# Where the first norm of token blocks 2 and 3 is taken: by tokens in place of by features

## The chip, the core and the metric

The program runs on one core of one Trainium2 chip. The metric is the device time of one execution in microseconds (us), taken as a median over runs. The core has a matrix engine (TensorE, PE in the profile), a vector engine (VectorE, DVE), a scalar engine (ScalarE, ACT), a general engine (GpSimd, POOL), and an engine that issues the transfers between HBM and the on-chip memory (SyncE, SP). The matrix engine writes into PSUM banks; everything else stays in SBUF tiles of 128 partitions.

## The reference

One layer of an encoder: stick-breaking attention (16 heads of 64) and a SwGLU feed-forward part, both between RMS norms and with shift, scale and gate from a conditioning vector. S = 2048 tokens, D = 1024 features, float32. The change touches only the first line:

```python
def rms_norm(x, g):
    return x * lax.rsqrt(jnp.mean(x * x, axis=-1, keepdims=True) + EPS) * g

h = modulate(rms_norm(x, norm_g[0]), sh_m, sc_m)      # h * (1 + scale) + shift
q, k, v = split(h @ w_qkv)
for each 128-token block:
    z = q k^T / 8;  sp = softplus(z) below the diagonal;  rest = reverse cumsum(sp)
    o = exp(z - rest) @ v
x = x + gate * rms_norm(o @ w_o, norm_g[1])
x = x + gate * rms_norm(swiglu_ffn(modulate(rms_norm(x, norm_g[2]), ...)), norm_g[3])
```

## The kernel before

**Tiling.** The tokens lie in four blocks of 512 (0 to 3), the heads in eight pairs p, the features in eight slices k of 128. Each float32 product is made of three matmuls over a high and a low half (`mm3`, L198 to L200): high by high, high by low, low by high. One product of a projection is a chain of 8 slices, 24 matmuls of 128x512, into one PSUM bank (`pj`).

**Steps.** The attention phase is a list of steps (p, b). `project` (L472) makes for each step three products: t=1 (keys), t=0 (queries), t=2 (values), in this order. The first steps are (0,0), then (1,0), which is "parked" (its keys, queries and values are written to HBM as `k_park`, `q_park`, `v_park` and read back later), then (0,1), (0,2), (0,3), and after them the other pairs. So step number 2 is block 1, step 3 is block 2, step 4 is block 3. Scores (`z`, L610), softplus (`a`, L627, and `z`, L629, on ACT), the running sums (`w`, L639 and L644 on DVE; `a`, L651 on POOL), turns of the weights (`t`, L661) and the products with the values (`o`, L689) are woven between the slices of the projections.

**The normalised input.** `first_norm(b, k)` (L435) makes for slice k of block b a high and a low half in an `ht` tile; each second slice is also stored to HBM (`h_s`), from where the other head pairs load it. Three slices of the next block are made during the product t=2 of the step before (`NORM_AT`), the other five during t=1 of the block's own step. Block 0 is loaded by tokens, squared on ACT with a running total per token (`rms_scale`, L186), scaled by DVE and turned by PE. Block 1 is loaded twice: by tokens for its squares, and by features (`xt`, `cols_load`, L322) for the values; the factor of each token is spread along a row (`x_spread`), turned into a row that every partition has (`x_share`), and multiplied in (`scale_cols`, L400; `modulate`, L410).

**Blocks 2 and 3 before.** They are loaded by features alone (`xc` tiles, 512 KB each, four to a block). Squares: ACT, one instruction of 128x1024 to a tile (`cols_square`, L341); the four tiles of squares are added up on POOL or DVE (`cols_add`, L347, then L349); the sum over the partitions is a matmul against ones (`cols_sum`, `xq`, L355), from which DVE and POOL make the factors (L359, L361). Then spread, share and `xv` (L369, L376, L381), and scaling: even slices on DVE (L404) then ACT (L415) and DVE (L416); odd slices on POOL (L408), then ACT (L420, L421) and DVE (L423).

**What sets the order.** PE, ACT, DVE and POOL run in the order in which the code is written. The table `X_AT` (key: step number, product, slice) places the pieces of the norms of blocks 2 and 3 into it. The transfers all go over SP; each waits for the one issued eight places ahead of it. A tile with a tag shares that tag's buffers (`BUFS`: `qt` 3, `kt` 7, `v` 7, `wraw` 2, `qkn` 2, `tmp` 4): a new tile waits until the tile that had the buffer before has been used up. The halves of the keys and queries of the parked step lie in the tag `wraw` (`split`, L509: `place = "wraw" if parked else "qkn"`) until `k_park` and `q_park` have been written out.

Of the kernel before, what the change touches and what calls it, by code (L numbers as in the profile page):

```python
# [16 lines left out]
P = 128  # L17
# [78 lines left out]

ON_GPSIMD = ((2, 1), (3, 1), (3, 2))
# [29 lines left out]
def hybrid_trunk_kernel(  # L127
# [25 lines left out]
    nc.vector.memset(lead, -0.5)  # L153
# [160 lines left out]
    x_pairs, x_squares, x_spreads = {}, {}, {}  # L314

    def x_load(b, i, tag="v"):
        tok = att.tile([P, D], F32, name=f"x{b}_{i}", tag=tag, bufs=BUFS[tag])
        r0 = b * BT + i * P
        nc.sync.dma_start(tok, x[r0 : r0 + P])
        x_tiles[b, i] = tok  # L320

    def cols_load(b, *which, tag="kt"):  # L322
        for m in which or range(KC // 2):
            cols = att.tile([P, 2, BT], F32, name=f"xc{b}_{m}", tag=tag, bufs=BUFS[tag])
            nc.sync.dma_start(cols, xt[b - 1, :, 2 * m : 2 * m + 2])
            x_pairs[b, m] = cols
            x_cols[b, 2 * m], x_cols[b, 2 * m + 1] = cols[:, 0], cols[:, 1]

    def x_square(b, i):
        junk = x_tiles[b, i]  # L330
        if b == 0:
            junk = x_norm[i] = att.tile([P, D], F32, name=f"xn0_{i}", tag="kt", bufs=BUFS["kt"])
        x_rstd[b, i] = rms_scale(att, x_tiles[b, i], f"n0_{b}_{i}", junk=junk)

    def cols_square(b, m):
        if m == 0 or (m == 2 and b == 2):
            both = att.tile([P, 2, 2, BT], F32, name=f"xs{b}_{m}", tag="qt", bufs=BUFS["qt"])
            x_squares.setdefault(b, []).extend([both[:, 0], both[:, 1]])
        elif m > 1 and b == 3:
            x_squares[b].append(x_squares[b][1])  # L340
        nc.scalar.activation(x_squares[b][m], x_pairs.pop((b, m)), AF.Square)  # L341

    def cols_add(b, m):
        total = x_squares[b][0]
        if m < KC // 2:
            engine = nc.gpsimd if (b, m) in ON_GPSIMD else nc.vector
            engine.tensor_tensor(total, total, x_squares[b][m], op=ALU.add)  # L347
        else:
            nc.vector.tensor_tensor(total[:, 0], total[:, 0], total[:, 1], op=ALU.add)  # L349

    def cols_sum(b):
        total = x_squares.pop(b)[0]
        ps = accps.tile([P, BT], F32, name=f"xq{b}", tag="acc")
        for i in range(4):
            nc.tensor.matmul(  # L355
                ps[:, i : i + 1], total[:, 0, i * P : (i + 1) * P], ones[:, 0:1], start=True, stop=True
            )
        ms = att.tile([P, 4], F32, name=f"xm{b}", tag="x_ms", bufs=1)
# [410 lines left out]
    def turn_x(m):  # L769
        turned_x[m] = x_turn(m)  # L770
# [1033 lines left out]
```

## Time and profile before

| | us |
|---|---|
| median of three runs | 2848.14 |
| the three runs | 2847.87, 2855.06, 2848.14 |
| the profiled execution | 2851.93 |
| its span in the trace | 2849.8 |
| PE busy in the span | 2802.1 (98%) |
| DVE, ACT, POOL busy | 2027.4, 1633.5, 1289.5 |

The span runs from the first to the last instruction in the trace; the profiled execution has 2.1 us outside it. Times in the text count from the span's start. The attention phase is about the first half; the pieces that the change moves lie between 40 and 160 us, around the steps of blocks 1, 2 and 3 of head pair 0. In the views, a row of the timeline gives start, length, engine, line, operation, output<-inputs and, in brackets, the idle time before it and what ended that. Names leave the buffer numbers out, so `xc` there may be a tile of any block.

### The profile page before, as it was taken

Reading aid. Unit: us, or ns where it says so; the run is one execution under the profiler, and the core shown is the slowest. Engines: PE = TensorE matmul, PEld = TensorE weight load, DVE = VectorE, ACT = ScalarE, POOL = GpSimd, SP = SyncE. Lnnn points to the kernel's source line nnn. Section 1 sums busy time; section 2 is a strip of 40 time slices with the busy share of each in tenths; the row PEclk is TensorE's granted clock in tenths of the full one; section 3 lists DMA queues with packets and bytes.
Section 4 is the critical chain, followed back from the end, with each engine's and each line's share of the span. In section 5 each row is a group of like instructions: output and inputs, shape, how many; then the busy total and the mean of one; then the engine's idle time right before and its main releaser. Section 6 shows DMA issues by size and latency. Waiting matters only on the chain.

```text
span 2849.8 us, 41730 instructions
## 1 busy us (share of the span) xinstructions
PE 2802.1 (98%) x13809; PEld 2334.5 (82%) x13809; DVE 2027.4 (71%) x2828; ACT 1633.5 (57%) x3268; POOL 1289.5 (45%) x2033
## 2 busy tenths in 40 slices
PE   9799999999999999999999999999999999999999
PEld 6688888888888888887887888888888888888887
DVE  7688898888888888888866866655776655124366
ACT  5587777788787777877645533333433333322243
POOL 1575666666576655657410222222222222544454
PEclk9899999999999999999999999999999999999999
DMA  9765647657565545637289645334553335545575
GB/s 361 251 211 165 198 140 243 197 174 236 173 221 198 188 138 170 211 117 243 69 304 308 214 137 159 111 92 153 159 168 117 111 98 172 191 133 153 181 225 192
DMA packets 239209, 518.94 MB, mean 182 GB/s; under 512 B 22417, under 2 KB 108433, under 8 KB 222098
## 3 DMA queue, kind: packets, MB, share of 16 engines
q1 hardware_dynamic: 238994, 516.28, 55.8%
q8 instruction: 109, 1.79, 0.3%
q14 instruction: 106, 0.87, 0.1%
HBM read 348.95 MB, written 118.49 MB: 164 GB/s over the span
## 4 chain that ended last, share of the span: by engine, by line
PE 86%; DVE 4%; DMA 3%; issue 2%; ACT 2%; POOL 1%; SPq 0%; DVEq 0%; POOLq 0%; ACTq 0%
PE s L198 9%; PE s L200 9%; PE s L199 9%; PE z L610 8%; PE o L689 8%; PE t L661 8%; PE pj L198 5%; PE pj L199 5%; PE pj L200 5%; PE o L199 5%; PE o L198 5%; PE o L200 5%; PE y L200 1%; PE y L198 1%; PE y L199 1%
## 5 line engine op out<-in xcount | busy, mean ns | idle before, releaser
L651 POOL TENSOR_TENSOR a<-a,w 128x512 f32<-128x512 f32 (+3 forms) x640 | 622.7, 973 | 219.5 <-DVE w L644 129.0
L644 DVE TENSOR_TENSOR_SCAN w<-z,c,begin 128x512 f32<-128x512 f32 x384 | 489.6, 1279 | 83.4 <-ACT z L629 61.9
L198 PE MATMUL s<-r,l 128*128 128x512 f32 x1232 | 481.5, 391 | 1.2 <-DVE p L1535 0.7
L200 PE MATMUL s<-r,l 128*128 128x512 f32 x1232 | 479.6, 389 | 0.0
L199 PE MATMUL s<-r,l 128*128 128x512 f32 x1232 | 479.4, 389 | 0.0
L627 ACT ACTIVATE a<-z 128x512 f32<-128x512 f32 (+3 forms) x640 | 347.1, 542 | 168.1 <-PE z L610 137.7
L689 PE MATMUL o<-aT,v 128*128 128x512 f32 (+3 forms) x1280 | 385.0, 382 | 0.1
L677 DVE TENSOR_TENSOR aT<-t,aT 128x512 fp32r<-128x512 f32 (+3 forms) x640 | 359.1, 595 | 23.7 <-ACT aT L671 23.1
L610 PE MATMUL z<-kt,qt 128*128 128x512 f32 (+3 forms) x1280 | 364.8, 366 | 4.6 <-DVE w L639 4.6
L671 ACT CAST aT<-t 128x512 fp32r<-128x512 f32 (+3 forms) x640 | 313.9, 533 | 74.4 <-PE t L661 64.5
L629 ACT ACTIVATE z<-z 128x512 f32<-128x512 f32 (+3 forms) x640 | 344.8, 539 | 0.0
L1543 POOL TENSOR_TENSOR one<-p,p 128x512 f32<-128x512 f32 x44 | 70.6, 1604 | 574.6 <-issue 304.4
L198 PE MATMUL pj<-ht,w 128*128 128x512 f32 x768 | 310.2, 404 | 6.0 <-issue 1.4
L661 PE MATMUL t<-begin,a 128*128 128x128 f32 x2176 | 296.3, 274 | 13.5 <-DVE aT L677 12.3
L661 PEld LDWEIGHTS t<-begin,a 128*128 128x128 f32 x2176 | 256.2, 141 | 63.9 <-DVE aT L677 14.2
L199 PE MATMUL pj<-ht,w 128*128 128x512 f32 x768 | 302.8, 394 | 4.3 <-DVE ht L416 3.5
L200 PE MATMUL pj<-ht,w 128*128 128x512 f32 x768 | 302.7, 394 | 0.0
L198 PEld LDWEIGHTS s<-r,l 128*128 128x128 f32 x1232 | 231.3, 188 | 51.2 <-DVE p L1535 1.5
L200 PEld LDWEIGHTS s<-r,l 128*128 128x128 f32 x1232 | 231.3, 188 | 48.6 <-DVE l L1397 0.4
L199 PEld LDWEIGHTS s<-r,l 128*128 128x128 f32 x1232 | 231.3, 188 | 48.0 <-issue 0.5
L610 PEld LDWEIGHTS z<-kt,qt 128*128 128x128 f32 x1280 | 231.4, 189 | 42.5 <-DVE w L639 5.2
L639 DVE TENSOR_TENSOR_SCAN w<-z,begin 128x128 f32<-128x128 f32 (+3 forms) x256 | 208.8, 818 | 76.3 <-ACT z L629 65.4
(184 smaller groups left out, 4882.2 us busy)
## 6 DMA issues: line engine op xcount, KB each, us to landing
ht<-h_s SPq DMA_DIRECT2D x108, 1024.0 KB, 8.0
wi<-in_win SPq DMA_DIRECT2D x86, 512.0 KB, 4.0
qt<-qn SPq DMA_DIRECT2D x124, 256.0 KB, 4.8
ol_qt<-act_s SPq DMA_DIRECT2D x56, 512.0 KB, 3.7
act_s<-S SPq DMA_DIRECT2D x66, 256.0 KB, 3.9
br<-in_wout SPq DMA_DIRECT2D x66, 256.0 KB, 3.6
h_s<-ht SPq DMA_DIRECT2D x16, 1024.0 KB, 8.0
o_s<-os SPq DMA_DIRECT2D x128, 128.0 KB, 2.9
```

What stands on the lines that cost most here:

```text
L198: nc.tensor.matmul(acc, lhs[0], rhs[0], start=first, stop=False, **kw)
L199: nc.tensor.matmul(acc, lhs[0], rhs[1], start=False, stop=False, **kw)
L200: nc.tensor.matmul(acc, lhs[1], rhs[0], start=False, stop=last, **kw)
L610: nc.tensor.matmul(z[:, :n], q[:, e, part, r * P : (r + 1) * P], k[:, e, :n], start=part == 0, stop=part == 1,)
L627: nc.scalar.activation(a[:, :n], z[:, :n], AF.Sigmoid, scale=QK_SCALE)
L629: nc.scalar.activation(z[:, :n], z[:, :n], AF.Sigmoid, scale=-QK_SCALE)
L644: nc.vector.tensor_tensor_scan(rest[:, rev], left[:, rev], begin[:, :BT][:, rev], initial=carries[r], op0=ALU.mult, op1=ALU.bypass,)
L651: nc.gpsimd.tensor_tensor(a[:, :n], a[:, :n], rest[:, 1 : n + 1], op=ALU.mult)
L661: nc.tensor.transpose(pt[:, rb * P : (rb + 1) * P], weighed[i, rb][:, j * P : (j + 1) * P], ident)
L671: nc.scalar.copy(hl[:, 0, t0:], pt[:, t0:])
L677: nc.vector.tensor_tensor(hl[:, 1, t0:], pt[:, t0:], f32(hl[:, 0, t0:]), op=ALU.subtract)
L689: nc.tensor.matmul(acc[:, t0:], lhs, hl[:, part, t0:], start=sc == qb and j == 0 and part == 0, stop=sc == 0 and j == 3 and part == 1,)
```

## The change

**Block 2** is loaded by tokens (`x_load(2, ...)`, four tiles of 128 tokens, two to a buffer of the tag `qt`), sooner in the code than its feature tiles were. It is squared by tokens on ACT as block 0 is, with the squares themselves written into a throw-away tile `xj` of the tag `wraw`; scaled in place by DVE (`x_scale`, 128x1024 each); turned by PE, four 128x128 transposes to a slice (`x_turn`), into the projections' PSUM banks (`accps`); and modulated by ACT straight from PSUM, with two instructions of DVE for the high and the low half. The square sums, the `xq` matmuls, the row and the feature scaling of block 2 go.

**Block 3** is loaded by tokens as well as by features, 2 MB more. It is squared by tokens in place during step 3, its factors are spread into the token tiles themselves, and the row is turned and copied as before, at (3, 0, 1) in place of (3, 0, 6). Its additions and its `xq` matmuls go; its scaling and modulation by features stay. Its feature tiles are loaded a step later, at (3, 1, 0).

**Block 1** is computed as before; its factors are spread into its token tiles. The constant `lead` (not used for the exponent any more) is 0.0 in place of -0.5.

```diff
+BY_FEATURES = (1, 3)
+
 X_AT = {
-    (2, 1, 1): [("load", 3)],
-    (2, 1, 3): [("square", 2, 0)],
-    (2, 1, 4): [("square", 2, 1), ("add", 2, 1)],
-    (2, 1, 5): [("square", 2, 2)],
-    (2, 1, 6): [("square", 2, 3), ("add", 2, 2)],
-    (2, 1, 7): [("add", 2, 3)],
-    (2, 0, 0): [("add", 2, 4)],
-    (2, 0, 5): [("sum", 2)],
-    (2, 0, 6): [("spread", 2)],
-    (2, 2, 0): [("share", 2)],
-    (2, 2, 3): [("square", 3, 0)],
-    (2, 2, 5): [("square", 3, 1)],
-    (2, 2, 7): [("add", 3, 1)],
-    (3, 1, 0): [("square", 3, 2)],
-    (3, 1, 2): [("add", 3, 2)],
-    (3, 1, 3): [("square", 3, 3)],
-    (3, 1, 5): [("add", 3, 3)],
-    (3, 1, 6): [("add", 3, 4)],
-    (3, 0, 1): [("sum", 3)],
-    (3, 0, 2): [("spread", 3)],
-    (3, 0, 6): [("share", 3)],
+    (2, 1, 4): [("square", 2, 0)],
+    (2, 1, 5): [("square", 2, 1)],
+    (2, 1, 6): [("square", 2, 2)],
+    (2, 1, 7): [("square", 2, 3)],
+    (2, 0, 0): [("scale", 2, 0), ("load", 3)],
+    (2, 0, 1): [("scale", 2, 1)],
+    (2, 0, 2): [("scale", 2, 2)],
+    (2, 0, 3): [("scale", 2, 3)],
+    (3, 1, 0): [("cols", 3), ("square", 3, 0)],
+    (3, 1, 1): [("square", 3, 1)],
+    (3, 1, 2): [("square", 3, 2), ("spread", 3, 0)],
+    (3, 1, 3): [("square", 3, 3), ("spread", 3, 1)],
+    (3, 1, 4): [("spread", 3, 2)],
+    (3, 1, 5): [("spread", 3, 3)],
+    (3, 0, 1): [("share", 3)],
 }
...
+    def x_load(b, *which, tag="v"):
+        for i in which or range(4):
+            r0 = b * BT + i * P
+            if b == 2:
+                if i % 2 == 0:
+                    x_places[b] = att.tile([P, 2, D], F32, name=f"x{b}_{i}", tag="qt", bufs=BUFS["qt"])
+                tok = x_places[b][:, i % 2]
+            else:
+                tok = att.tile([P, D], F32, name=f"x{b}_{i}", tag=tag, bufs=BUFS[tag])
+            nc.sync.dma_start(tok, x[r0 : r0 + P])
...
+        elif b == 2:
+            junk = att.tile([P, D], F32, name=f"xj{b}_{i}", tag="wraw", bufs=BUFS["wraw"])
         x_rstd[b, i] = rms_scale(att, x_tiles[b, i], f"n0_{b}_{i}", junk=junk)
...
+    def x_scale(b, i):
+        nc.vector.tensor_scalar(x_norm[b, i], tok, x_rstd.pop((b, i)), None, op0=ALU.mult)
+
+    def x_spread(b, i):
+        nc.vector.tensor_scalar(x_tiles[b, i][:, :P], ones, x_rstd.pop((b, i)), None, op0=ALU.mult)
...
     def modulate(hl, b, k):
...
+        if b not in BY_FEATURES:
+            u = att.tile([P, BT], F32, name=f"hf{b}_{k}", tag="tmp", bufs=BUFS["tmp"])
+            nc.scalar.activation(u, x_turn(b, k), AF.Identity, bias=add, scale=gain)
+            nc.vector.tensor_copy(hl[:, 0], u)
+            nc.vector.tensor_tensor(hl[:, 1], u, f32(hl[:, 0]), op=ALU.subtract)
+            return
...
+    x_load(2, 0, 1)
     store(2)
...
+    cols_load(1, 3)
     full(7)
     high(7)
-    cols_load(1, 3)
-    cols_load(2, 0, 1, tag="v")
+    x_load(2, 2, 3)
```

**What this moves on ACT**, from the values of the two first steps to the first instruction after block 1's keys and queries (`v0`, `v1`: values; `xs2`: squares of `xc2`; `kn`, `qn`: split of keys and queries; DMAHW names one of SP's eight semaphores). Before:

```order
50 L562 CAST v0_0_722<-vt0_0_717 128x8x64 [waits PE_49]
51 L341 ACTIVATE xs2_0_725<-xc2_0_565 128x1024 [waits DMAHW1_49]
52 L341 ACTIVATE xs2_0_725<-xc2_1_567 128x1024 [waits DMAHW2_49]
53 L562 CAST v1_0_740<-vt1_0_735 128x8x64 [waits PE_49]
54 L341 ACTIVATE xs2_2_744<-xc2_2_584 128x1024 [waits DMAHW4_49]
55 L341 ACTIVATE xs2_2_744<-xc2_3_601 128x1024 [waits DMAHW5_49]
56 L512 CAST kn0_1_758<-pj0_1_1_685 128x512 [waits DMAHW1_49,DMAHW6_49,DMAHW0_49,DMAHW7_49,PE_49,Activation_49]
57 L512 CAST qn0_1_806<-pj0_1_0_766 128x512 [waits DMAHW3_49,DMAHW4_49,DMAHW2_49,DMAHW5_49,PE_49,Activation_49]
58 L381 COPY xv2_820<-xr2_815 128x512 [waits PE_49]
```

After:

```order
50 L540 CAST v0_0_711<-vt0_0_706 128x8x64 [waits PE_49]
51 L183 ACTIVATE xj2_0_717,n0_2_0_ssq_718<-x2_0_509 128x1024 [waits DMAHW7_49,DMAHW6_49,Activation_49]
52 L540 CAST v1_0_732<-vt1_0_727 128x8x64 [waits PE_49]
53 L183 ACTIVATE xj2_1_736,n0_2_1_ssq_737<-x2_0_509 128x1024 [waits DMAHW0_49,Activation_49]
54 L183 ACTIVATE xj2_2_746,n0_2_2_ssq_747<-x2_2_568 128x1024 [waits DMAHW7_49,DMAHW3_49]
55 L183 ACTIVATE xj2_3_756,n0_2_3_ssq_757<-x2_2_568 128x1024 [waits DMAHW4_49,Activation_49]
56 L490 CAST kn0_1_766<-pj0_1_1_682 128x512 [waits DMAHW1_49,DMAHW0_49,PE_49]
57 L490 CAST qn0_1_811<-pj0_1_0_774 128x512 [waits DMAHW4_49,DMAHW3_49,DMAHW5_49,DMAHW2_49,PE_49]
58 L387 ACTIVATE hf2_0_830<-xT2_0_831,mod_75,g_eff_73 128x512 [waits PE_49]
```

The squares keep their place. The first one waited for its load alone; now it waits for two transfers, its load and the one that last read the buffer of its throw-away tile: `xj2_0` takes the place in `wraw` of `kn1_0`, which `k_park` reads, and `xj2_2` that of `qn1_0`, which `q_park` reads. The next two instructions after the split of the keys and queries are now on turned slices.

**On PE**, at the end of block 1's queries and the first slice of its values (`xr2`: the row; `z0`: the first score of pair 0 against block 0's keys). Before:

```order
236 L200 MATMUL pj0_1_0_766<-ht0_1_3_708,w0_0_302 128x512
237 L376 MATMUL xr2_815<-begin_62,xw2_795 128x128 x4
238 L198 MATMUL pj0_1_2_814<-ht0_1_0_603,w0_2_317 128x512
239 L199 MATMUL pj0_1_2_814<-ht0_1_0_603,w0_2_317 128x512
240 L200 MATMUL pj0_1_2_814<-ht0_1_0_603,w0_2_317 128x512
241 L198 MATMUL pj0_1_2_814<-ht0_1_0_603,w0_2_317 128x512
242 L199 MATMUL pj0_1_2_814<-ht0_1_0_603,w0_2_317 128x512
243 L200 MATMUL pj0_1_2_814<-ht0_1_0_603,w0_2_317 128x512
244 L610 MATMUL z0_0_828<-kt0_0_655,qt0_0_666 128x128 x2
245 L198 MATMUL pj0_1_2_814<-ht0_1_1_648,w0_2_317 128x512
```

After:

```order
238 L194 MATMUL pj0_1_0_774<-ht0_1_3_697,w0_0_302 128x512
239 L192 MATMUL pj0_1_2_819<-ht0_1_0_600,w0_2_317 128x512
240 L193 MATMUL pj0_1_2_819<-ht0_1_0_600,w0_2_317 128x512
241 L194 MATMUL pj0_1_2_819<-ht0_1_0_600,w0_2_317 128x512
242 L192 MATMUL pj0_1_2_819<-ht0_1_0_600,w0_2_317 128x512
243 L193 MATMUL pj0_1_2_819<-ht0_1_0_600,w0_2_317 128x512
244 L194 MATMUL pj0_1_2_819<-ht0_1_0_600,w0_2_317 128x512
245 L588 MATMUL z0_0_826<-kt0_0_652,qt0_0_663 128x128 x2
246 L366 MATMUL xT2_0_831<-begin_62,x2_0_509 128x128 x2
247 L366 MATMUL xT2_0_831<-begin_62,x2_2_568 128x128 x2
248 L192 MATMUL pj0_1_2_819<-ht0_1_1_645,w0_2_317 128x512
```

The row's transposes are gone from in front of block 1's values, and the `xq` matmuls from two slices further up (they stood between two slices of `pj0_1_0`); the first turn of block 2 stands behind the first score. The other seven turns follow, one to a slice or two, up to slice 4 of block 2's keys.

**On SP**, around the parked keys. Before:

```order
36 L325 DMA xc2_0_565<-in_xt 128x1024
37 L325 DMA xc2_1_567<-in_xt 128x1024
38 L794 DMA h_s0_83<-ht0_0_3_517 128x2048
39 L325 DMA xc2_2_584<-in_xt 128x1024
40 L325 DMA xc2_3_601<-in_xt 128x1024
41 L529 DMA kt0_0_655<-kn0_0_652 64x512 x4
42 L545 DMA qt0_0_666<-qn0_0_663 64x1024 x4
43 L524 DMA k_park_81<-kn1_0_673 128x1024
44 L538 DMA q_park_80<-qn1_0_677 128x1024
```

After:

```order
34 L319 DMA x2_0_509<-in_x 128x1024 x2
35 L772 DMA h_s0_83<-ht0_0_2_448 128x2048
36 L325 DMA xc1_3_563<-in_xt 128x1024
37 L319 DMA x2_2_568<-in_x 128x1024 x2
38 L772 DMA h_s0_83<-ht0_0_3_520 128x2048
39 L507 DMA kt0_0_652<-kn0_0_649 64x512 x4
40 L523 DMA qt0_0_663<-qn0_0_660 64x1024 x4
41 L502 DMA k_park_81<-kn1_0_670 128x1024
42 L516 DMA q_park_80<-qn1_0_674 128x1024
```

Block 2's four loads stand ahead of the store of block 0's last slices, two of them also ahead of the store before it; the same transfers as before stand ahead of `k_park`. Behind `q_park` block 3's four loads by features stood ahead of `v_park`; now its four loads by tokens stand behind the first copy of block 1's keys, and those by features behind block 1's queries.

More of the change, by code (lines that the diff above doesn't have):

```diff
@@ L152, in hybrid_trunk_kernel @@
     lead = const.tile([P, 112], F32, name="lead")
-    nc.vector.memset(lead, -0.5)
+    nc.vector.memset(lead, 0.0)
     begin = const.tile([P, BT + 1], F32, name="begin")
@@ L331, in x_square @@
         if b == 0:
-            junk = x_norm[i] = att.tile([P, D], F32, name=f"xn0_{i}", tag="kt", bufs=BUFS["kt"])
+            junk = x_norm[b, i] = att.tile([P, D], F32, name=f"xn{b}_{i}", tag="kt", bufs=BUFS["kt"])
+        elif b == 2:
+            junk = att.tile([P, D], F32, name=f"xj{b}_{i}", tag="wraw", bufs=BUFS["wraw"])
         x_rstd[b, i] = rms_scale(att, x_tiles[b, i], f"n0_{b}_{i}", junk=junk)
[L335 to L358, printed above, removed]
-        nc.vector.tensor_scalar(ms, ps[:, :4], 1.0 / D, EPS, op0=ALU.mult, op1=ALU.add)
-        rstd = att.tile([P, 4], F32, name=f"xd{b}", tag="x_rstd", bufs=1)
-        nc.gpsimd.tensor_tensor(rstd, ms, lead[:, :4], op=ALU.pow)
-        x_rstd[b] = rstd
@@ L364, in x_spread @@
-    def x_spread(b, *which):
-        if b not in x_spreads:
-            x_spreads[b] = att.tile([P, 4, P], F32, name=f"xw{b}", tag="tmp", bufs=BUFS["tmp"])
-        for i in which or range(4):
-            rstd = x_rstd[b][:, i : i + 1] if b > 1 else x_rstd.pop((b, i))
-            nc.vector.tensor_scalar(x_spreads[b][:, i], ones, rstd, None, op0=ALU.mult)
+    def x_scale(b, i):
+        tok = x_tiles.pop((b, i))
+        if b > 0:
+            x_norm[b, i] = tok
+        nc.vector.tensor_scalar(x_norm[b, i], tok, x_rstd.pop((b, i)), None, op0=ALU.mult)
```

60 lines of the change are left out of this document (26 added, 34 removed).

## The prediction, made before the changed kernel was run

> **What bounds the kernel now.** I read the page's head first, then the stretches of 20 us, to find where the matrix engine isn't full.
>
> ```profile
> span 2849.8 us, 41730 instructions
> PE 2802.1 (98%) x13809; PEld 2334.5 (82%) x13809; DVE 2027.4 (71%) x2828; ACT 1633.5 (57%) x3268; POOL 1289.5 (45%) x2033
> 60.00:80.00 20.00, 17.32 (x80) 14.09 (x79) 13.01 (x21) 9.78 (x15) 4.74 (x4) 0.91 0.99 337
> 80.00:100.00 20.00, 11.58 (x44) 8.43 (x43) 12.01 (x15) 13.73 (x25) 10.24 (x12) 0.83 1.01 336
> 100.00:120.00 20.00, 18.22 (x85) 14.47 (x85) 15.16 (x23) 10.03 (x23) 11.20 (x20) 0.83 0.66 245
> ```
>
> PE is busy for 2802 of 2850 us, so what the change does off PE's path is worth nothing. A stretch gives PE, weight load, DVE, ACT and POOL, then the granted clock, the DMA share and GB/s. The change acts where PE has holes: 2.7, 8.4 and 1.8 us idle in these three, at a clock of 0.91, 0.83 and 0.83. In two of them the DMA engines are full. PE's waits from 50 to 260 us (us in total, times, longest):
>
> ```profile
> PE t L661 <- DVE aT L677: 5.9, 4, 2.3
> PE z L610 <- DVE w L639: 4.6, 1, 4.6
> PE pj L199 <- DVE ht L416: 3.5, 2, 2.3
> PE xq L355 <- DVE xs L349: 3.1, 2, 2.7
> ```
>
> The last three lie inside this span of 60 us. The first lies behind it (127 us on), where the order is the same in both kernels: I leave it as it is. PE's timeline gives the marks:
>
> ```profile
> 69.55 0.39 PE L200 MATMUL pj<-ht,w 128*128 128x512 f32 x1
> 72.62 1.06 PE L355 MATMUL xq<-ones,xs 128*128 128x1 f32 x8 [2.68 <-DVE xs L349]
> 74.98 0.63 PE L198 MATMUL pj<-ht,w 128*128 128x512 f32 x1
> 75.40 0.63 PE L199 MATMUL pj<-ht,w 128*128 128x512 f32 x1
> 79.11 0.33 PE L610 MATMUL z<-kt,qt 128*128 128x128 f32 x2
> 79.28 0.45 PE L198 MATMUL pj<-ht,w 128*128 128x512 f32 x1
> 83.62 0.39 PE L199 MATMUL pj<-ht,w 128*128 128x512 f32 x1
> 83.84 0.40 PE L200 MATMUL pj<-ht,w 128*128 128x512 f32 x1
> 88.86 1.22 PE L610 MATMUL z<-kt,qt 128*128 128x512 f32 x2 [4.62 <-DVE w L639]
> 99.77 0.50 PE L199 MATMUL pj<-ht,w 128*128 128x512 f32 x1 [2.33 <-DVE ht L416]
> 104.22 0.80 PE L199 MATMUL pj<-ht,w 128*128 128x512 f32 x1 [1.12 <-DVE ht L416]
> 109.01 0.33 PE L610 MATMUL z<-kt,qt 128*128 128x128 f32 x2
> 109.72 1.02 PE L355 MATMUL xq<-ones,xs 128*128 128x1 f32 x8 [0.38 <-DVE xs L349]
> ```
>
> Starts of matmuls are 0.22 to 0.23 us apart at full clock (83.62, 83.84) and 0.42 to 0.43 at half (74.98, 75.40). After each long wait the half rate lasts for 4 to 6 us, so a wait costs itself and some 2 us more. I follow the change through three marks that both kernels have: the second slice of block 1's values (79.28), the last score of the first unit (88.86), the first score behind block 2's keys (109.01).
>
> **ACT and the queue.** What ends last ahead of these marks stands on ACT and SP:
>
> ```profile
> 64.30 2.01 ACT L341 ACTIVATE xs<-xc 128x1024 f32<-128x1024 f32 x2
> 68.80 1.06 ACT L341 ACTIVATE xs<-xc 128x1024 f32<-128x1024 f32 x1 [1.05 <-DMA xc<-in_xt]
> 70.55 0.59 ACT L512 CAST kn<-pj 128x512 fp32r<-128x512 f32 x1 [0.69 <-DMA kt<-kn]
> 85.34 1.06 ACT L341 ACTIVATE xs<-xc 128x1024 f32<-128x1024 f32 x1 [4.08 <-DMA xc<-in_xt]
> 103.65 1.06 ACT L341 ACTIVATE xs<-xc 128x1024 f32<-128x1024 f32 x1 [4.44 <-POOL w L624]
> 69.43 0.45 SPq L524 DMA_DIRECT2D k_park<-kn  x1
> k_park<-kn SPq DMA_DIRECT2D x1, 512.0 KB, 4.7
> q_park<-qn SPq DMA_DIRECT2D x1, 512.0 KB, 5.4
> v_park<-v SPq DMA_DIRECT2D x1, 512.0 KB, 13.5
> ```
>
> The squares of block 2 now run from 64.30. In the changed order the first of them also waits until `k_park` has read the buffer that its throw-away tile takes. `k_park` is issued at 69.43 and needs 4.7 us: it lands at 74.1. The bytes ahead of it are the same in the change, so I keep that time. The first square thus starts 9.8 us later than before, not sooner, whatever its load does. Behind it on ACT stand the parked step's second value cast, three squares and the split of block 1's keys, then that of its queries; behind the keys' split on DVE, the four scalings.
>
> **The change part by part.** Durations:
>
> ```profile
> L189 ACT ACTIVATE x<-x 128x1024 f32<-128x1024 f32 x4 | 4.2, 1052 | 0.0
> L389 DVE TENSOR_SCALAR xn<-x,n_rstd 128x1024 f32<-128x1024 f32 x4 | 3.0, 749 | 0.0
> L395 PE MATMUL xT<-begin,xn 128*128 128x128 f32 x32 | 4.6, 272 | 0.0
> L774 ACT ACTIVATE hf<-xT,mod,g_eff 128x512 f32<-128x512 f32 x8 | 6.2, 778 | 13.4 <-DVE g_eff L740 12.4 <-PE xT L395 0.9
> L789 DVE TENSOR_TENSOR ht<-hf,ht 128x512 fp32r<-128x512 f32 x8 | 5.5, 686 | 1.6 <-ACT ht L785 1.6
> L627 ACT ACTIVATE a<-z 128x384 f32<-128x384 f32 x5 | 2.5, 507 | 0.6 <-PE z L610 0.6
> L347 POOL TENSOR_TENSOR xs<-xs 128x1024 f32<-128x1024 f32 x3 | 7.6, 2526 | 16.2 <-ACT xs L341 16.2
> ```
>
> *First mark.* Removed ahead of it: the wait for the sums (2.68), the sums (0.9), their half-rate matmuls, the row's transposes. PE stops at 69.78 before (69.55 + 0.23); fifteen matmuls (9 of the queries' last slices, 6 of the values' first) of 0.23 and the first score, 0.17, remain: it stands at the first turn at 73.4. That turn needs the four scaled tiles: 74.1 + four squares 4.2 + the value cast and the keys' cast (0.59 each, by the row of the latter) = 79.5; + DVE's half of the split 0.69 + four scalings 3.0 = 83.2; + one turn of four transposes (32 in 4.6: 0.58) = 83.8. So PE has one hole of 9.8 us where it had 2.7, and the mark moves from 79.28 to 83.8: 4.5 late. For comparison, without the wait for `k_park` the same chain from 68.8 (where the last load of block 2 came before) ends about 78.5.
>
> *Second mark.* Before, 18 matmuls and two small scores lead to a wait of 4.62: ACT stood at 85.34 behind a square of block 3 whose load wasn't there, and the first scores' softplus behind it. In the change block 3's squares stand behind the unit's first three scores, so this wait has no cause: the softplus of the first score follows the second turned slice, at about 87, and its buffer is free by about 89. What remains is work: 10 matmuls at half rate (0.43 each, 4.3, as long as the spells before), 8 at full rate (1.8), two turns (4.6 for the eight of block 0: 0.58 each, 1.2), two scores (0.7): 8.0 us, with the turn at half rate 8.2. The mark moves from 88.86 to 92.0: 3.1 late.
>
> *Third mark.* Before, 20.15 us (88.86 to 109.01), with waits for the halves of block 2 (2.33, 1.12) and 4.44 us of ACT behind POOL, which has the 2.5-us additions in front of what ACT needs. In the change POOL has none, and ACT is what sets the pace: from 92.0 the copy of the values 0.6, the softplus of two scores 1.8, the cast of the values 0.6, five turned slices (5 x 0.78 = 3.9), four squares of block 3 (4.2), the fourth score and a first one (1.2 + 0.5): 12.8. Some 1 us of the copy and the first softplus lies ahead of the mark: 11.8, so the last turned slice ends at 103.8. DVE makes its halves in 1.2 (0.69 and a copy, by the nearest row 0.69, at best half of it), and six matmuls follow: 106.4. PE's own work between these marks is shorter at full clock: 27 matmuls of 0.23 (6.2), five turns of 0.58 (2.9), some 1.5 for the values' and the first weights' turns (11 transposes, at 0.145 as in a turn) and 1.2 for scores make 11.8 against 14.4. The mark moves from 109.01 to 106.4: 2.6 early. Its cover: block 3's token loads must be in by 94 to 103. They stand behind the first copy of block 1's keys, whose split ends at 80.2 (79.5 + 0.69), and by the 11.4 us of loads in this stretch the first lands at about 92 or a little later, its square being due at 94 behind the third turned slice. The new copy of block 1's queries must wait for the last turn (it takes a buffer of block 2's tokens) and lands at about 105: just in time for the first score.
>
> ```profile
> xc<-in_xt SPq DMA_DIRECT2D x12, 512.0 KB, 11.4
> qt<-qn SPq DMA_DIRECT2D x8, 256.0 KB, 6.8
> ```
>
> *Behind the marks.* The second sums (0.38 and 1.02) go, block 3's row comes in their place (0.58) and is missing where it was: 1.4 less. Block 3's two POOL additions and its spreads lie under other work, and the 2 MB more of loads stand in a stretch where the DMA share has fallen to 0.66. I cost these at nothing; if a feature tile of block 3 came late, the wait would show at the marks of step 4, at up to 2 us as the waits for `ht` here.
>
> *The sum.* -2.6 - 1.4 = -4.0, the lighter POOL and DVE behind the marks at nothing. Of the profiled execution's 2851.93 that leaves 2847.9; of the median 2848.14, which lies 3.8 below it, 2844.1. The bounds: the turned slices' DVE copy at half or whole (0.3 to 0.7 each, five of them), the half-rate stretch a window of some 3.5 us earlier or later (1.7 either way), and the transfers (below). I take 2844, and 2839.5 to 2848.5 for this case by itself.
>
> A rule of the Trainium skill speaks against my 8.2 us of the second mark: "TensorE: Matmul & The Clock Gate", Part 4: PE-mode transpose, says that transposes do not count as busy for the clock gate the way matmuls do. By it the half rate would last one window longer among the turns, and the sum would be up to 1.7 us higher, by the half window that the bounds above give for it (estimate, 2845.8). The trace does not settle it: no turn in it follows a long wait.
>
> **The rivals.** *The transfers are slower (ends slower).* Mechanism: `k_park` is now what block 2 waits for, and the row of `v_park`, of the same 512 KB, shows 13.5 us in the next stretch with the DMA share at 1.01. Should `k_park` take that, it lands at 82.9, the first turn and all behind it moves by 8.8, the copy of the queries (5.4 to 6.8 us behind the last turn) adds up to 3.3 and one more half-rate window 1.7: -4.0 + 8.8 + 3.3 + 1.7 = +9.8, 2858. It decides from a landing at about 78 on (then the gain is used up); +0.3% needs about 82. For it: a share of 0.99 to 1.01, and ACT's squares in front of everything. Against: 4.7 and 5.4 measured, behind the same bytes.
>
> *The transfers are quicker (faster).* Block 2's loads stand further up in SP's order, so the queue may be through sooner: between 60 and 80 the DMA share is just under full at 337 GB/s. Should `k_park` land 5 us sooner, at 69, all three marks come about 5 earlier, and the half-rate stretch, begun in the middle of block 1's values, is no longer: -4.0 - 5.1 = -9.1, 2839. For it: the hole is one chain, and each us there is one of the whole. Against: the DMA engines are full in both stretches, so the bytes ahead set the time.
>
> *It does what it says (squares sooner).* If the throw-away tile did not wait for `k_park`, squares from 64 to 69 would end the chain of the first mark 5 us sooner as well (78.5 in place of 83.2): 2839. Against it stands the wait in the order; I count it with the quicker case.
>
> **How the numbers follow.** A measurement of this kernel tells about 0.3% (8.5 us) from no change: faster means below 2839.6, slower above 2856.7. My case has 0.42: 0.30 of it within, 0.07 below and 0.05 above, since every row behind the first mark is an estimate of an order that hasn't run. The slower case has 0.34, 0.29 of it above the line. The two quicker ones have 0.24 together; both lie close to the line, and what comes sooner at the first mark may also fall on one window less of half rate: 0.23 below. Faster 0.30, same 0.36, slower 0.34. Cases of both signs hold most of the chance: mine by itself has 2839.5 to 2848.5, and the range for 8 in 10 takes in the quicker case with one window less and the slower one: 2835 to 2859.
>
> **What would show it.** Right: PE waits for a scaled tile at the first turn, 8 to 11 us long, ending at about 83; ACT's first square of block 2 starts within 1 us of `k_park`'s landing; no `xq`; no wait of over 1 us at the last score of the first unit; the first score behind block 2's keys at 105 to 108. Wrong: a first square at 64 to 69 (the wait is not there), a landing of `k_park` past 78, a wait of PE for the queries' copy at about 105 or for block 3's token loads on ACT, and any new wait after 120 us, where I have put nothing.

## The result, and the profile after

The changed kernel takes 2839.91 us (median of five runs, 2837.15 to 2840.45) against 2849.58 for the kernel before (five runs, 2847.87 to 2856.61). The ratio is 0.9957 with a 95% interval of 0.9945 to 0.9968: faster by 0.43%, some 9.7 us by the medians. The profiled execution took 2840.45 with a span of 2838.2.

The head of the page of the changed kernel, and its stretches of 20 us (PE, weight load, DVE, ACT, POOL, granted clock, DMA share, GB/s):

```profile
span 2838.2 us, 41766 instructions
PE 2798.2 (99%) x13821; PEld 2331.5 (82%) x13821; DVE 2022.4 (71%) x2833; ACT 1630.7 (57%) x3271; POOL 1282.5 (45%) x2032
60.00:80.00 20.00, 15.03 (x69) 11.79 (x67) 10.36 (x20) 9.62 (x18) 2.25 (x5) 0.93 1.02 377
80.00:100.00 20.00, 18.80 (x93) 14.41 (x93) 15.23 (x31) 15.16 (x32) 6.60 (x14) 0.90 0.93 319
100.00:120.00 20.00, 18.40 (x101) 15.48 (x100) 15.74 (x25) 13.83 (x32) 10.51 (x22) 1.00 0.94 318
```

The hole, the stretch in which PE stands idle, has moved forward. From 60 to 80 us PE is idle for 5.0 us (2.7 before), from 80 to 100 only for 1.2 (8.4 before), and the clock of the last two stretches is 0.90 and 1.00 in place of 0.83 twice. PE's waits from 50 to 260 us in the changed kernel:

```profile
PE t L639 <- DVE aT L655: 5.9, 4, 2.3
PE xT L366 <- DVE x L340: 5.2, 4, 4.6
```

The first row is the one that both kernels have behind 110 us. The waits for the sums, for the running sums and for block 2's halves (2.7 + 0.4, 4.6 and 3.5 before) are gone; one wait for the scaled tiles has come. PE's timeline at the marks of the prediction, and the row of a later mark, seven turns of weights (`t`) that both kernels make behind the same wait:

```profile
73.38 0.33 PE L588 MATMUL z<-kt,qt 128*128 128x128 f32 x2
78.31 0.48 PE L366 MATMUL xT<-begin,x 128*128 128x128 f32 x1 [4.60 <-DVE x L340]
80.30 0.47 PE L366 MATMUL xT<-begin,x 128*128 128x128 f32 x1 [0.19 <-DVE x L340]
80.43 0.78 PE L192 MATMUL pj<-ht,w 128*128 128x512 f32 x1
84.28 0.40 PE L193 MATMUL pj<-ht,w 128*128 128x512 f32 x1
87.86 0.62 PE L588 MATMUL z<-kt,qt 128*128 128x512 f32 x2
101.79 0.34 PE L588 MATMUL z<-kt,qt 128*128 128x128 f32 x2
118.42 0.96 PE L639 MATMUL t<-begin,a 128*128 128x128 f32 x7 [1.60 <-DVE aT L655]
```

And ACT, SP and the transfer that the hole hangs on:

```profile
71.66 1.06 ACT L183 ACTIVATE xj<-x 128x1024 f32<-128x1024 f32 x1 [7.06 <-issue]
66.02 0.53 SPq L502 DMA_DIRECT2D k_park<-kn  x1
k_park<-kn SPq DMA_DIRECT2D x1, 512.0 KB, 5.6
```

| mark | before | changed | difference |
|---|---|---|---|
| second slice of block 1's values | 79.28 | 80.43 | +1.15 |
| last score of the first unit | 88.86 | 87.86 | -1.00 |
| first score behind block 2's keys | 109.01 | 101.79 | -7.22 |
| seven weight turns behind their wait of 1.6 | 127.36 | 118.42 | -8.94 |

The row of the last mark in the kernel before:

```profile
127.36 0.95 PE L661 MATMUL t<-begin,a 128*128 128x128 f32 x7 [1.61 <-DVE aT L677]
```

So the first turn is reached late, as the wait for `k_park` makes it, and what lies behind it is quicker than before. The first square starts at 71.66, when `k_park` has landed (66.02 + 5.6). The spans differ by 11.6 us, 2.7 more than the marks show. The rest lies behind the marks, most of it around 1540 us, in code that is the same in both kernels: from the last mark to the first product of the feed-forward part it is 1449.7 us in the profiled execution of the kernel before and 1446.1 in that of the changed kernel, but it also lies anywhere from 1444.2 to 1449.3 in those of the experiments, and at 1446.0 in one whose code there is that of the kernel before. It varies by the execution; the medians' 9.7 agrees with the marks.

### The profile page after: what moved, and what is told of

Same layout as the page of the kernel before. It is cut to its first block, busy times and chain, and to the rows that moved or that the text cites. A ratio compares the mean times of both kernels' runs of the same rounds, so it can differ in the third digit from the quotient of the medians.

```text
span 2838.2 us, 41766 instructions
## 1 busy us (share of the span) xinstructions
PE 2798.2 (99%) x13821; PEld 2331.5 (82%) x13821; DVE 2022.4 (71%) x2833; ACT 1630.7 (57%) x3271; POOL 1282.5 (45%) x2032
## 4 chain that ended last, share of the span: by engine, by line
PE 88%; DVE 4%; issue 2%; DMA 2%; ACT 2%; POOL 1%; SPq 0%; DVEq 0%; POOLq 0%; ACTq 0%
PE s L192 9%; PE s L193 9%; PE s L194 9%; PE z L588 8%; PE o L667 8%; PE t L639 8%; PE pj L192 5%; PE pj L194 5%; PE pj L193 5%; PE o L194 5%; PE o L193 5%; PE o L192 5%; PE y L194 2%; PE y L192 2%; PE y L193 2%
## 5 line engine op out<-in xcount | busy, mean ns | idle before, releaser
L649 ACT CAST aT<-t 128x512 fp32r<-128x512 f32 (+3 forms) x640 | 313.9, 533 | 73.6 <-PE t L639 63.5
```

Of the source, the lines that this page charges most:

```text
L649: nc.scalar.copy(hl[:, 0, t0:], pt[:, t0:])
```

## The experiments

The stage is measured here from the second turn of values (`vt`, at 63.85 before and 64.05 in the changed kernel) to the seven weight turns of the last mark. For both kernels: 127.36 - 63.85 = 63.5 and 118.42 - 64.05 = 54.4 us.

| kernel | second `vt` at | stage | median | ratio to before, interval |
|---|---|---|---|---|
| before | 63.9 | 63.5 | 2849.58 | |
| changed | 64.1 | 54.4 | 2839.91 | 0.9957 (0.9945 to 0.9968) |
| changed, second time | 64.0 | 54.7 | 2842.00 | 0.9962 (0.9948 to 0.9975) |
| throw-away tile elsewhere | 64.0 | 52.8 | 2837.73 | 0.9953 (0.9941 to 0.9966) |
| block 2 alone | 64.6 | 61.6 | 2850.13 | 0.9998 (0.9989 to 1.0007) |
| loads late | 65.3 | 55.0 | 2842.83 | 0.9976 (0.9966 to 0.9986) |
| before, squares of block 3 later | 73.1 | 63.9 | 2850.21 | 1.0002 (0.9993 to 1.0011) |
| tile elsewhere, squares of block 3 later | 68.3 | 52.4 | 2840.46 | 0.9963 (0.9951 to 0.9975) |
| before, one square of block 3 | 63.7 | 53.3 | 2838.86 | 0.9961 (0.9949 to 0.9973) |
| changed, squares of block 3 later | 64.0 | 53.9 | 2840.33 | 0.9961 (0.9950 to 0.9973) |
| queries' copy free | 72.0 | 46.1 | 2835.37 | 0.9939 (0.9927 to 0.9951) |
| the same, second time | 64.9 | 47.4 | 2833.11 | 0.9937 (0.9924 to 0.9949) |
| before, additions on DVE | 65.1 | 61.9 | 2848.60 | 0.9993 (0.9984 to 1.0001) |
| before, squares later and additions on DVE | 72.1 | 58.7 | 2850.09 | 0.9992 (0.9983 to 1.0002) |

Where the second column is over 68, the profiled execution had lost 4 to 9 us before the stage (the last section says to what); the transfers had that much more time there, so such a stage flatters the kernel and the median is the better measure. The kernel before was run beside each set (medians of 2849.58 to 2851.94), so the ratios compare kernels of different sets better than the medians do; where two intervals overlap, the two kernels are not told apart.

**The throw-away tile in another tag.** 

```diff
-            junk = att.tile([P, D], F32, name=f"xj{b}_{i}", tag="wraw", bufs=BUFS["wraw"])
+            junk = att.tile([P, D], F32, name=f"xj{b}_{i}", tag="v", bufs=BUFS["v"])
```

> The changed kernel, with the throw-away tile of block 2's squares in the tag v, so that the squares no longer wait for k_park. If the wait for k_park makes the hole ahead of the first turn (4.6 + 0.6 us in the changed kernel): the first square starts at 64 to 65 in place of 71.66, the split of block 1's keys ends at about 71.8 (its cast then waits for the copy of the earlier keys, as before the change, at about 70.5), four scalings end at about 74.8, PE waits 1.3 to 2 us at the first turn, the half-rate spell is gone, and the time is about 2833 to 2835. If the time there is given back later, since block 3's token loads and the copy of block 1's queries come no sooner: the first mark is early too, but the third one hardly, and the time is 2838 to 2840. If something else made the hole: no change, 2840.

Measured: the first square starts at 64.48 and PE has no wait at the first turn; the second mark comes at 79.64 (87.86 in the changed kernel). Then most of it is given back. Two rows of this kernel's ACT and one of PE's waits:

```profile
64.48 1.06 ACT L183 ACTIVATE xj<-x 128x1024 f32<-128x1024 f32 x1
88.94 1.06 ACT L183 ACTIVATE x<-x 128x1024 f32<-128x1024 f32 x1 [6.45 <-DMA x<-in_x]
```

```profile
PE xT L366 <- ACT hf L387: 6.5, 1, 6.5
```

ACT reaches block 3's first square at 82.5 and its token tile lands at 88.9. The third mark comes at 100.19, 1.6 sooner than in the changed kernel; the median is 2.2 lower, which the intervals don't tell apart. So the wait for `k_park` does make the hole; and it hid another, the load of block 3's tokens. The second of the three expectations had the course of it right (its 2838 to 2840 ended 0.3 above the median).

**Block 2 alone.** Block 3's squares, additions, sums and loads by features as before the change, at their old keys; block 2 turned.

```diff
+    (2, 1, 1): [("cols", 3)],
...
+    (2, 2, 3): [("csquare", 3, 0)],
+    (2, 2, 5): [("csquare", 3, 1)],
+    (2, 2, 7): [("add", 3, 1)],
+    (3, 1, 0): [("csquare", 3, 2)],
...
```

> Block 2 turned as in the change, block 3's norm by features as before (its squares, additions, sums and the place of its loads); block 2's token tiles lie in the tag v. If block 3's feature squares on ACT (behind loads that are not there) and its additions on POOL were half of what was lost before: a wait of PE of 1 to 4 us comes back between 85 and 100, the third mark (first score behind block 2's keys, 101.8 in the changed kernel) moves to 104 to 107, and the time is 2843 to 2848. If the gain is all block 2's: third mark within 1 us, time 2839 to 2841.

Measured: no gain at all, 0.9998. The hole at the first turn is there, and behind it ACT stands at block 3's feature squares again, for their load and for POOL's additions:

```profile
84.82 1.06 ACT L366 ACTIVATE xs<-xc 128x1024 f32<-128x1024 f32 x1 [2.40 <-DMA xc<-in_xt]
93.46 1.06 ACT L366 ACTIVATE xs<-xc 128x1024 f32<-128x1024 f32 x1 [1.87 <-POOL w L655]
100.89 1.06 ACT L366 ACTIVATE xs<-xc 128x1024 f32<-128x1024 f32 x1 [3.02 <-POOL w L655]
```

The third mark is at 108.68, where it was 109.01 before and 101.79 in the changed kernel. The stage is 1.9 us shorter than before, and the time is the same: turning block 2 alone buys nothing that can be measured, and the changed kernel's gain comes only with block 3's part, which the first alternative held for half of it. No run has block 3 by tokens and block 2 by features, so what block 3's part is worth alone was not measured; the next experiment shows what the pieces cost that it removes.

**The kernel before, without block 3's squares and additions.**

```diff
-    (2, 2, 3): [("square", 3, 0)],
-    (2, 2, 5): [("square", 3, 1)],
-    (2, 2, 7): [("add", 3, 1)],
-    (3, 1, 0): [("square", 3, 2)],
-    (3, 1, 2): [("add", 3, 2)],
-    (3, 1, 3): [("square", 3, 3)],
-    (3, 1, 5): [("add", 3, 3)],
+    (3, 1, 5): [("square", 3, 0)],
...
         total = x_squares[b][0]
+        if b == 3:
+            return
```

> The kernel before with three of the four squares and all additions of block 3 left out and the one square left at (3, 1, 5), so that block 3's factors come from one tile of the feature squares alone. If block 3's feature squares on ACT and their additions on POOL, which wait for one another and for the loads, are what the second half of the gain came from: the waits at the last score of the first unit and at block 2's slices in 88 to 105 fall to under 2 us together, and the time is 2841 to 2845. If not, 2848 to 2850.

Measured: 2838.86, below the range expected and as much as the whole change gains, with block 2 by features as before. This kernel leaves work out that a complete one must do in some form, so it shows what these pieces cost and not what a replacement would take. Its waits:

```profile
PE xq L351 <- DVE xs L345: 2.7, 1, 2.7
PE pj L193 <- DVE ht L412: 2.3, 1, 2.3
```

The wait of 4.62 at the last score and that of 1.12 are gone; the one for block 2's sums is still there. Three squares (3.2 us of ACT) and the additions cost the kernel 11.6 us (2850.49 in the same set, less 2838.86). ACT's order has block 3's squares between the slices of block 2 and between the scores' softplus, so what a square waits for holds these up too.

**Two ways to mend block 3 by features.** The first two squares and their addition at the start of step 3:

```diff
-    (2, 2, 3): [("square", 3, 0)],
-    (2, 2, 5): [("square", 3, 1)],
-    (2, 2, 7): [("add", 3, 1)],
-    (3, 1, 0): [("square", 3, 2)],
+    (3, 1, 0): [("square", 3, 0), ("square", 3, 1), ("add", 3, 1), ("square", 3, 2)],
```

> The kernel before, with one edit: the first two squares of block 3 and their addition stand in front of the third square, at the start of step 3. If ACT behind the load of block 3 made the wait of 4.62 us at the last score of the first unit: that wait is gone, the second mark moves from 88.86 to 84 to 85, some of it is given back where ACT then waits for the additions on POOL ahead of the next slices of block 2, and the time is 2845 to 2848 against 2849.6. If another work ends last there (the running sums on DVE): the wait stays over 2 us and the time too.

The additions on DVE:

```diff
-ON_GPSIMD = ((2, 1), (3, 1), (3, 2))
+ON_GPSIMD = ((2, 1),)
```

> The kernel before with block 3's first two additions on DVE in place of POOL. If POOL's additions (2.4 to 2.8 us each, behind POOL's scaling of block 2) are what ACT's third and fourth square stood behind (0.33 and 4.44 us before): the wait of 4.44 falls under 2, the waits of PE for L416 and L423 (2.33, 1.12) shrink, and the time is 2845 to 2848 against 2850.5; the wait of 4.62 for the load stays. If DVE, which has block 2's scaling and the running sums there, is as late: 2849 to 2852.

And both together:

> The kernel before with block 3's first two squares at the start of step 3 (as in the fourth experiment) and its first two additions on DVE. If load and additions each made a wait and the one edit only moved the stall to the other: both go, the time is 2842 to 2846. If the late squares are themselves what is too much there for ACT and DVE: 2848 to 2851.

Measured: 2850.21, 2848.60 and 2850.09, none clear of the kernel before. With the squares later the wait of 4.62 is gone, but ACT stands twice behind the additions, and PE waits for it in their place (ACT's rows, then PE's):

```profile
102.55 1.06 ACT L338 ACTIVATE xs<-xc 128x1024 f32<-128x1024 f32 x1 [2.45 <-POOL w L621]
111.98 1.06 ACT L338 ACTIVATE xs<-xc 128x1024 f32<-128x1024 f32 x1 [4.44 <-POOL w L621]
```

```profile
105.26 0.79 PE L195 MATMUL pj<-ht,w 128*128 128x512 f32 x1 [5.55 <-ACT ht L412]
```

With the additions on DVE and the squares where they were, the row of the fourth square reads:

```profile
102.81 1.06 ACT L341 ACTIVATE xs<-xc 128x1024 f32<-128x1024 f32 x1 [3.37 <-DVE xs L347]
```

3.37 us in place of 4.44: it isn't only POOL that is slow. With both edits ACT waits 1.29 and 3.35 us for the additions on DVE, and PE once for ACT:

```profile
100.05 0.51 PE L195 MATMUL pj<-ht,w 128*128 128x512 f32 x1 [4.35 <-ACT ht L412]
```

The third and fourth squares go into the one buffer that the addition before must have read, and that addition stands behind block 2's scaling on whichever engine it is. By these rows the loop from ACT to the addition and back holds ACT in all three kernels, and with it the scores and slices behind.

**The loads' place.** The changed kernel with block 2's token loads where its feature loads were.

```diff
-    x_load(2, 0, 1)
     store(2)
...
-    cols_load(1, 3)
...
-    x_load(2, 2, 3)
+    cols_load(1, 3)
+    x_load(2, 0, 1)
...
     store(3)
+    x_load(2, 2)
...
     x_share(1)
+    x_load(2, 3)
```

> The changed kernel with block 2's token loads at the places in the code where its feature loads stood before the change. If the place of these loads is what brought k_park 2.5 us sooner (its issue waits, through the copies of the first queries, for the transfer eight places ahead, which is then the last of block 2's loads): k_park is issued at about 69.4 and lands at about 74, all three marks move 2.5 us back and the time is about 2842 to 2843. If the bytes ahead set it whatever their order: k_park at 66 and 71.6 as in the changed kernel, time 2840.

Measured: 2842.83, within the first range expected; it is 2.9 above the changed kernel's first median and 0.8 above its second, and the intervals overlap. `k_park` is issued at 68.50 and the hole is 5.34 + 0.57 us (4.60 + 0.56 in the changed kernel), but PE also reaches it 1.2 later in this execution. The copies of the first queries, which SP issues ahead of `k_park`, wait for block 2's loads here and in the kernel before; SP's waits from 57 to 70 us, of this kernel and then of the one before:

```profile
SPq L523 <- DMA x<-in_x: 4.0, 2, 2.0
```

```profile
SPq L545 <- DMA xc<-in_xt: 4.9, 3, 2.1
```

In the changed kernel SP shows no wait for these loads there. So the place of the loads is a cause; its share is open, with one execution of each. By the time in the span, `k_park` is issued at 66.02 in the changed kernel, 68.50 here and 69.43 before: the place is 2.5 of the 3.4 us. Counted from the second turn of values, which comes 1.2 us later here, it is issued 2.0, 3.2 and 5.6 us behind that turn: the place is a third.

**Block 3's token squares later.** Behind the turns of block 2, once in the changed kernel and once with the throw-away tile elsewhere:

```diff
-    (3, 1, 0): [("cols", 3), ("square", 3, 0)],
-    (3, 1, 1): [("square", 3, 1)],
-    (3, 1, 2): [("square", 3, 2), ("spread", 3, 0)],
-    (3, 1, 3): [("square", 3, 3), ("spread", 3, 1)],
+    (3, 1, 0): [("cols", 3)],
+    (3, 1, 5): [("square", 3, 0)],
+    (3, 1, 6): [("square", 3, 1)],
+    (3, 1, 7): [("square", 3, 2), ("spread", 3, 0)],
+    (3, 0, 0): [("square", 3, 3), ("spread", 3, 1)],
...
-    (3, 0, 1): [("share", 3)],
+    (3, 0, 6): [("share", 3)],
```

> The changed kernel with block 3's squares and row as late as in the other run of this call, its throw-away tile where the change has it. There ACT never waits for block 3's loads, since the hole at the first turn gives them time, so only the four squares (4.2 us of ACT) leave the stretch up to the third mark, which PE's own work of some 12 us then bounds: third mark 99.5 to 101 in place of 101.8 and 2838 to 2840. If the order of the squares itself is worth more, 2835 to 2837.

> The first experiment's kernel (throw-away tile in the tag v) with block 3's four squares in the slices 5 to 7 of block 2's keys and the first of its queries (behind the turns of block 2) and the row at (3, 0, 6). If the 6.5 us that ACT stood behind block 3's token loads there took back the gain: no wait of PE over 1 us between 73 and 95, the third mark (100.2 there) comes to 94 to 96, bounded by the copies of block 1's queries, which are issued behind the last turn, and the time is 2831 to 2834. If those copies or POOL's running sums end last: a new wait of 3 to 6 us at the first score behind block 2's keys, and 2836 to 2838.

Measured: in the changed kernel no difference (2840.33; third mark 100.73 in place of 101.79). The squares did not leave the stretch ahead of that mark, as was expected: they stand behind the turns now, but three of the four still start ahead of it (95.88, 96.91 and 99.23). With the tile elsewhere the 6.5 us of ACT are gone, and PE's waits have a new row:

```profile
PE z L589 <- DMA qt<-qn: 3.6, 1, 3.6
```

The copies of block 1's queries are issued at 90.98, behind the last turn, whose token tile has their buffer, and the first score waits for them. That is the wait of the second expectation; the median, 2840.46, lies over both ranges and is no better than with the tile moved alone.

**A buffer for the queries' copy.** In the kernel with the tile elsewhere and the squares later, two of block 2's token tiles in the tag `v`, two of block 3's in `wraw`.

```diff
-            if b == 2:
+            if b == 2 and i < 2:
...
-                tok = att.tile([P, D], F32, name=f"x{b}_{i}", tag=tag, bufs=BUFS[tag])
+                place = "wraw" if b == 3 and i < 2 else tag
+                tok = att.tile([P, D], F32, name=f"x{b}_{i}", tag=place, bufs=BUFS[place])
```

> The kernel with the throw-away tile elsewhere and block 3's squares late, with two of block 2's token tiles in the tag v in place of qt and two of block 3's in wraw, so that the copy of block 1's queries needs no buffer that the last turn must free. If that buffer made the wait of 3.6 us (and the half rate behind it): no wait of PE for qt, the first score behind block 2's keys comes 2 to 3.6 us sooner against the first score of block 1's values (23.4 us between them in the run before, now 20 to 21.5), and the time falls by 3 to 5 us against 2840.5, to 2835 to 2838. If SP's queue in front of these copies (block 3's loads, two stores) sets it: the same wait, 2840.

Measured: 2835.37 and no wait for `qt`, but with a late start. So it ran again, beside the changed kernel:

> The same kernel as the one that freed the copies of block 1's queries, beside the changed kernel on one chip; its first profile had lost 8 us to half rate ahead of the stage, which gave the transfers time that they do not have otherwise. If the free buffer is what removed the wait for the queries' copy: with a start like the changed kernel's (second turn of values at 64) PE still waits under 1 us for qt, the first score behind block 2's keys comes at 94 to 96, and the kernel is 4 to 8 us quicker than the changed one. If only the late start hid that wait: 2 to 4 us of waiting are back at that score, and it is within 3 us of the changed kernel.

> The changed kernel itself, unedited, on the same chip as the kernel above, to compare the two directly. By the runs so far: 2838 to 2842, the first turn's hole 4 to 5.5 us, and a span from the first score of block 1's values to the first score behind block 2's keys of 28 to 29 us.

Measured: 2833.11 against 2842.00 on one chip, 8.9 us, for the three edits together. Marks and waits of the second run of the version:

```profile
80.54 0.62 PE L590 MATMUL z<-kt,qt 128*128 128x512 f32 x2
95.61 0.41 PE L590 MATMUL z<-kt,qt 128*128 128x128 f32 x2 [1.58 <-DVE x L345]
112.34 0.96 PE L641 MATMUL t<-begin,a 128*128 128x128 f32 x7 [1.60 <-DVE aT L657]
```

The copies are issued from 85.86 on (95.62 in the changed kernel). The 1.6 us of waiting that are left at that score are put down to DVE (the spread of block 3's factors); the copies, 9.0 us from issue to landing there, come in at much the same time, and which is last was not separated. The version is at 0.9937 (0.9924 to 0.9949) of the kernel before, the changed kernel beside it at 0.9962 (0.9948 to 0.9975): the intervals only just touch.

## Why the prediction was right, and where it was short

The time lay in the range, on the side that the forecast had, but the gain was 9.7 us where 4 were forecast. The range was 24 us wide, since it took in rivals of both signs. The quicker rival had a gain of 9.1, close to the one measured, but for a landing 5 us sooner; the landing came 2.5 sooner, and the rest is made of smaller errors that happened to have the same sign. By the steps of the forecast:

- *The squares wait for `k_park`, and are not sooner.* Right: 71.66, with the landing. Moving the tile (first experiment) removes the hole.
- *`k_park` lands at 74.1, since the bytes ahead are the same.* Wrong by 2.5: it landed at 71.6. This is half of the rival "the transfers are quicker", which had 5. The bytes were the same and their places were not; the loads' place is a third to three quarters of it, by what it is counted from.
- *The chain behind it.* From the landing to the end of the scalings 9.1 us were forecast. From 71.66 to 80.30, where the last tile's transpose starts, it took 8.6, and three of the four transposes ran under the scalings. The first mark came at 80.43 and not 83.8: 3.4 sooner, of which 2.5 are the landing and 0.9 this chain.
- *Second stretch, 8.2.* 7.43. The half rate ended at 84.28, after seven matmuls and a turn in place of the ten matmuls that I had given it. It lasted 3.9 us from the first of these matmuls, and 6.0 us from the first transpose ahead of them (78.31); behind the two long waits of the kernel before (2.68 and 4.62) it lasted some 4 and 5. The Trainium skill ("TensorE: Matmul & The Clock Gate", Part 4: PE-mode transpose) says that transposes do not count as busy for the clock gate the way matmuls do; these figures leave open whether that is so here.
- *Third stretch, 14.4, ACT's chain.* 13.93: near in size, but the path was wrong. PE's own work was put at 11.8 us; the profile has it busy for 12.91 of this stretch, at a granted clock of 1.00, and all its waits there come to about 1 us, of which 0.35 are for ACT (a turn at 95.12). With the squares behind the turns the stretch is 13.33, with PE busy for 12.51. So PE's own work all but fills it, and ACT's chain sets little of it. The stretch in the changed kernel, then with its squares later:

```profile
87.86:101.79 13.93, 12.91 (x70) 9.57 (x68) 12.91 (x27) 13.11 (x27) 6.82 (x14) 1.00 0.93 297
```

```profile
87.40:100.73 13.33, 12.51 (x69) 9.64 (x68) 12.59 (x23) 12.25 (x25) 4.65 (x11) 1.00 0.98 325
```

- *Behind the marks, -1.4.* -1.7 (118.42 against 127.36, less the third mark's 7.22).

The sum of these: 3.4 + 0.8 + 0.5 + 0.3 = 5.0 more than the forecast 4.0, which is the 9.0 that the marks show. The step that was short is the first mark, by its landing. Of the five signs named for a right forecast three came (the first square with the landing, no `xq`, no wait at the last score of the first unit); two did not: the wait at the first turn is 5.2 us and ends at 80.3, where 8 to 11 and 83 were named, and the third mark comes at 101.79, where 105 to 108 were.

Of the reasons, one was right in kind and wrong in place: I named POOL's additions as what ACT stood behind. On DVE they hold it nearly as long (3.37 for 4.44), and without POOL's first two additions the time doesn't change. By the kernel that leaves them out, what held ACT was block 3's feature squares and additions together, also with two of the squares later, with a shared buffer and a load in front. One thing I did not see: turning block 2 is worth nothing by itself. It exchanges one wait of 2.7 us and the sums for one of 5.2 and eight turns; in the changed kernel the gain comes with block 3's norm by tokens. The third case, squares that don't wait, was put at 5 us; the first experiment makes it, and its 2.2 are not clear of noise, since block 3's loads take the gain back. The slower rival did not come: `k_park` took 5.6, not 13.5, and `v_park` behind it 9.8.

## What to carry to other kernels

A throw-away output needs a buffer like any other: look at who last read the buffer that it gets, since a transfer there makes the instruction wait for something that it has no use for. An instruction that fills a pause of its own engine can cost several times its length, if it waits for a load or for another engine's result: here three squares of 1.06 us and their additions cost 11.6. When one wait is removed, find the next load, buffer or engine due behind it before the gain is counted; here the first edit behind the change gave 2.2 us and the second none, neither clear of noise, and only the three together gave 8.9.

## What the hardware showed that was not expected

The granted clock of the matrix engine can fall to half in a stretch that the profile counts as busy, and stay there for 12 us. Four of the 14 profiled executions, of four different kernels, show half rate between 24 and 36 us (0.50 to 0.66 on average), where no edit has begun to act. This is the row of the kernel before with the squares of block 3 later, then that of the changed kernel:

```profile
24.00:36.00 12.00, 12.00 (x40) 9.81 (x41) 5.93 (x12) 3.86 (x6) 0.00 (x0) 0.50 1.03 408
```

```profile
24.00:36.00 12.00, 12.00 (x59) 9.64 (x60) 11.05 (x20) 6.10 (x8) 0.00 (x0) 1.00 1.02 407
```

The profile has PE busy for all of the 12 us in both, at a granted clock of 0.50 and of 1.00, and the stage begins at 73.1 and 64.1. But not all of that is wide matmuls. In the first row 4.8 us of it are matmuls of a single column:

```profile
L722 PE MATMUL acol<-c_act,ar 128*128 128x1 f32 x22 | 4.8, 345 | 0.0
```

The last group of these ends at about 31 us, and the full rate is back at about 37. Such groups alone don't bring the half rate about: in the run with the loads late, two of them lie between 21 and 26 us at a granted clock of 1.00. The Trainium skill ("TensorE: Matmul & The Clock Gate", What's actually happening) has the full rate come after one busy window of about 3.4 us. Whether the first row disagrees depends on whether matmuls of one column count as busy there, and no run here shows that. What such a start costs, 4 to 9 us, is up to as much as the whole change is worth: before two traces are compared at a stage, compare where the stage begins.
